# The sums of w2 in an FFN's input stage, and the ring of operands in its output stage

## The chip, the cores and the metric

One core of a Trainium2 chip runs the whole program in one launch. Its engines are TensorE (PE, matrix products), VectorE (DVE), ScalarE (ACT), GpSimd (POOL) and SyncE (SP); in this kernel SP issues nearly all DMAs, on one queue. Each engine works through its own instructions in order, and engines wait for each other by semaphores. The metric is the device time of one execution in microseconds (us); times before are the median of three runs.

## The reference

One layer of a two-pass (context and denoising) backbone. What matters here is its last third, the SwiGLU FFN over T = 1280 tokens (256 of the context, 1024 of the sample) with D = 1024 and D_FF = 2816:

```python
    x = x + g1 * rmsnorm(m, lp['g_post1'])
    h = rmsnorm(x, lp['g_pre2']) * (1.0 + sc2) + sh2
    f = (jax.nn.silu(h @ lp['ffn_w1']) * (h @ lp['ffn_w3'])) @ lp['ffn_w2']
    x = x + g2 * rmsnorm(f, lp['g_post2'])
```

All of it is float32. The token mixers ahead of it are the same before and after.

## The kernel before

Each float32 operand is split in two parts, a rounded high part and the rest, the low part, and each product is three matmuls: high x high, high x low, low x high. `split` does this: L65 casts the high part on ACT, L66 subtracts it on DVE (or POOL) to get the low part. So a low part is ready only after its high part.

Both stages of the FFN use Strassen's scheme in Winograd's form: seven products of blocks instead of eight, with sums of blocks before and after.

The *input stage*, `ffn_in`, goes over the 22 column tiles of D_FF in 11 pairs f. Per pair there are two halves, one for w1 and one for w3. A half is one call of `products` (matmuls L1347 for the seven products, 512 wide, and L90 to L92 for the remaining 256 tokens, about 134 matmuls in all); the adds that take its products out of PSUM are DVE's L1352, on tiles `t`. `w_raw` loads the weights (L1294), `w_sums` forms their sums for the next half (L1313, L1315 and L1322 on DVE, L1324 on POOL). After a pair, the activations and their seven sums go to DRAM in `actd` (stores L1417, L1448, L1449).

The second operand of the output stage also needs sums, those of w2. They don't depend on anything computed: `w2_sums(f, q)` loads two tiles of 256 KB (L1460) into the pool `tmp`, makes four DVE operations of 128 x 256 (L1462 to L1465) on them and stores both to `w2t` in DRAM (L1467). The pool `tmp` has two buffers, so a call's loads wait for the stores of the call before. There are 22 calls, two per pair; in the code both stand between the halves of their pair. A scheduler orders each engine's instructions by its own estimate of when they can run, so that an instruction written late can be placed early.

The *output stage*, `ffn_out`, has seven products of 11 steps, one step per pair, called 0, 1, 4, 5, 3, 6 and last 2. A step takes one tile pair `op` (high and low, 640 columns of activations and 512 of w2) and makes 15 matmuls (L1504), three for each of five PSUM banks `pg` and `pm`. `operands` makes these tiles: load both parts into `raw` (L1494 from `actd`, L1495 from w2 or `w2t`; three buffers), then `split`. Steps 0 and 1 of product 0 are loaded early and in parts through another pool, s4. The pool `op` has 22 tiles, that is 11 steps. Between products the banks are emptied: ACT copies them to the accumulators after product 0 (L1517) and product 1, DVE adds after the others.

The last product holds all its 11 steps (`xs`) and goes bank by bank, so that each bank's rows can be finished by `final` while the next runs: gate row (`gate_row`, L1285), the residual x1d (load L1577, into s4), the norm and the store of the output.

Of the kernel before, what the change touches and what calls it, by code (L numbers as in the profile page):

```python
# [11 lines left out]
F32R = mybir.dt.float32r  # L12
# [29 lines left out]
class Builder:  # L42
# [1291 lines left out]
    def products(self, ops, w, t3, func11, early=False):  # L1334
# [44 lines left out]
        product(c, "s4", "b22", False)  # L1379
        add(u2, u2, c)  # L1380
        yield d

    def ffn_in(self, given):
# [4 lines left out]
        for f in range(0, FT, 2):  # L1388
            early = not f
            if raw:  # L1390
                wa = self.w_sums(raw)
# [24 lines left out]
            def out(i, src, cols=slice(0, 512)):  # L1416
                nc.sync.dma_start(self.actd[f // 2][:, i, cols], src)  # L1417

            for q in range(2):
                self.w2_sums(f // 2, q)  # L1420
            if not early:
                tb = three()
                pb = self.products(ops, w1, tb, mul11)
            *_, d = pb
            out(0, s11)
            tt = nc.vector.tensor_tensor
# [23 lines left out]

    def w2_sums(self, f, q):


        nc = self.nc
        tt = nc.vector.tensor_tensor
        src = self.a["w2"][2 * f * P:(2 * f + 2) * P, :].rearrange("(i p) (h q c) -> i q p h c", i=2, h=2, q=2)
        dst = self.w2t[f].rearrange("p (i j) (q c) -> i q p j c", i=2, q=2)
        x = [self.tmp() for _ in range(2)]
        for i in range(2):
            nc.sync.dma_start(x[i].rearrange("p (h c) -> p h c", h=2), src[i, q])  # L1460
        (b11, b12), (b21, b22) = ([y[:, :256], y[:, 256:]] for y in x)
        tt(b11, b12, b11, ALU.subtract)  # L1462
        tt(b12, b22, b12, ALU.subtract)
        tt(b22, b22, b11, ALU.subtract)
        tt(b21, b21, b22, ALU.subtract)  # L1465
        for i in range(2):
            nc.sync.dma_start(dst[i, q], x[i].rearrange("p (j c) -> p j c", j=2))  # L1467

    def ffn_out(self):
# [12 lines left out]
        def operands(i, b, early=False):  # L1482
            for f in range(FT // 2):
                hi, lo = (self.opp.tile([P, HALF + 512], F32R, tag="op", bufs=22, name=self.nm("op")) for _ in range(2))
                ca, cb = slice(0, HALF), slice(HALF, HALF + 512)
                if early and f < 2:
                    for src, c in ((self.actd[f][:, i], ca), (b[f], cb)):
                        raw = self.s4()
                        n = c.stop - c.start
                        nc.sync.dma_start(raw[:, :n], src)  # L1490
                        self.split(raw[:, :n], hi[:, c], lo[:, c])
                else:
                    raw = self.opp.tile([P, HALF + 512], F32, tag="raw", bufs=3, name=self.nm("raw"))
                    nc.sync.dma_start(raw[:, ca], self.actd[f][:, i])  # L1494
                    nc.sync.dma_start(raw[:, cb], b[f])  # L1495
                    self.split(raw, hi, lo)
                yield hi, lo
# [18 lines left out]
        for x, y in zip(B[0], ps):  # L1516
            acopy(x, y)  # L1517
        product(1, w2(1, first), ps, False)
        for x, y in zip(A[0], ps):
            acopy(x, y)  # L1520
# [11 lines left out]
        product(6, w2(1, second), ps, False)  # L1532
        g2s = [self.gate_row(1, s) for s in range(2)]
        for j, (t, y) in enumerate(zip(HALVES[0], ps)):
            add(A[1][j], A[1][j], y)
            self.final(t, acc[t], g2s[t // 8])
        ps = banks()
        xs = list(operands(2, t4))
        for j, t in enumerate(HALVES[1]):
# [34 lines left out]
    def final(self, t, acc, g2):  # L1574
        nc = self.nc
        x = self.s4()
        nc.sync.dma_start(x, self.x1d[t * P:(t + 1) * P, :])  # L1577
        rs = self.tiny.tile([P, 1], F32, tag="rs", bufs=6, name=self.nm("rs"))
# [126 lines left out]
```

## Time and profile before

| | us |
|---|---|
| median of three runs | 1661.93 (1661.32 to 1664.87) |
| the profiled execution | 1657.5 |
| its span in the trace | 1655.6 |
| PE busy in the span | 1511.2 (91%) |
| DVE busy | 1048.9 (63%) |
| ACT busy | 667.6 (40%) |
| mean granted clock of PE | 0.962 of full speed |

The profiled execution is 4.4 us faster than the median, and 1.9 us of it lie outside the span. The FFN takes the second half of the span: input stage from about 784 us to 1363.33, output stage from there to the end.

A row of a timeline gives start, duration, engine, line, operation and tiles, and in brackets how long the engine idled before it and what ended that. A matmul's duration overlaps that of the next, so starts tell the rate. A row of waits gives the waiting instruction, what it waited for, the total, how many times and the longest. Idle time counts only on the engine that the others wait for; here that is PE.

### The profile page before, as it was taken

To read this page: it belongs to the slowest core of one execution; us is meant where nothing else is said; L and a number is where in the kernel's file an instruction comes from. 1 tells how busy PE (TensorE), PEld (TensorE's weight loads), DVE (VectorE), ACT (ScalarE), POOL (GpSimd) and SP (SyncE) were. 2 spreads that over 40 slices of the span, in tenths; PEclk is the share of its full clock that TensorE was granted. 3 is DMA by queue.
4 is the path that set the end of the run, shared out by engine and by line. 5 is a ranking of instruction groups with operands and counts; after the bars stand their busy time and mean duration, and the time that the engine had idled before them with its cause. 6 is when DMAs were issued, how large, how long until landed. Compare 5 with 4: busy or idle time off the path is not lost.

```text
span 1655.6 us, 23292 instructions
## 1 busy us (share of the span) xinstructions
PE 1511.2 (91%) x8493; PEld 1245.3 (75%) x8493; DVE 1048.9 (63%) x1762; ACT 667.6 (40%) x1224; POOL 415.9 (25%) x416
## 2 busy tenths in 40 slices
PE   5999998889989979984988989999999998799997
PEld 2688778677677767873777778888888886688886
DVE  7776568997388996469666665555455534534555
ACT  5754244554456667455221222222222213433341
POOL 2333236555045665344010101101011000000003
PEclk9999998999999989996999999999999999999999
DMA  8434562444512454631566553222232338755544
GB/s 323 142 125 139 170 182 80 140 138 146 195 64 83 147 180 155 227 112 49 159 198 200 161 175 107 82 87 76 84 101 84 104 96 286 231 171 173 174 140 165
DMA packets 163226, 242.17 MB, mean 146 GB/s; under 512 B 34613, under 2 KB 97407, under 8 KB 162984
## 3 DMA queue, kind: packets, MB, share of 16 engines
q1 hardware_dynamic: 163112, 240.69, 44.8%
q8 instruction: 67, 1.10, 0.3%
q14 instruction: 47, 0.39, 0.1%
HBM read 169.05 MB, written 71.58 MB: 145 GB/s over the span
## 4 chain that ended last, share of the span: by engine, by line
PE 46%; DMA 11%; DVE 9%; issue 3%; ACT 3%; POOL 2%; SPq 1%; DVEq 0%; POOLq 0%; ACTq 0%
PE pg L1347 13%; PE pg L1504 7%; PE pm L1504 7%; PE pm L1347 5%; DMA tmp<-in_w 4%; DMA w2t<-tmp 4%; PE pg L90 2%; PE pg L92 2%; PE pg L91 2%; PE pm L92 2%; PE pm L90 2%; PE pm L91 2%; DMA raw<-in_w 2%; PE pm L1042 1%; DMA s<-in_wfm 1%
## 5 line engine op out<-in xcount | busy, mean ns | idle before, releaser
L66 DVE TENSOR_TENSOR op<-raw,op 128x1152 fp32r<-128x1152 f32 x75 | 101.8, 1358 | 122.3 <-ACT op L65 121.8
L90 PE MATMUL pg<-hh,s 128*128 128x512 f32 (+1 forms) x432 | 158.0, 367 | 3.9 <-ACT s L65 3.9
L92 PE MATMUL pg<-hh,s 128*128 128x512 f32 (+1 forms) x432 | 154.9, 363 | 7.1 <-DVE s L66 7.1
L91 PE MATMUL pg<-hl,s 128*128 128x512 f32 (+1 forms) x432 | 155.8, 361 | 0.6 <-POOL hl L204 0.6
L65 ACT CAST op<-raw 128x1152 fp32r<-128x1152 f32 x75 | 87.1, 1161 | 158.2 <-PE pg L1504 65.3
L1324 POOL TENSOR_TENSOR sr<-s,s 128x512 f32<-128x512 f32 x22 | 28.7, 1307 | 473.0 <-DVE sr L1322 447.1
L1347 PE MATMUL pg<-hh,su 128*128 128x512 f32 x352 | 121.7, 407 | 14.9 <-DVE t L1352 10.9
L65 ACT CAST su<-sr 128x512 fp32r<-128x512 f32 x88 | 53.9, 619 | 194.9 <-POOL sr L1324 98.9
L1504 PE MATMUL pg<-op,op 128*128 128x512 f32 x396 | 124.6, 397 | 5.2 <-DVE op L66 5.2
L65 ACT CAST s<-s 128x1024 fp32r<-128x1024 f32 (+2 forms) x67 | 69.6, 1038 | 136.9 <-DMA s<-in_w 101.2
L1347 PE MATMUL pg<-b1h,s 128*128 128x512 f32 x352 | 118.9, 400 | 5.5 <-DVE tmp L1565 4.5
L98 POOL TENSOR_TENSOR rs<-rs,mhalf 128x1 f32<-128x1 f32 x40 | 30.0, 753 | 368.5 <-DVE rs L97 367.5
L1504 PE MATMUL pm<-op,op 128*128 128x512 f32 x374 | 116.2, 392 | 0.0
L66 DVE TENSOR_TENSOR s<-s,s 128x1024 fp32r<-128x1024 f32 (+2 forms) x67 | 84.8, 1266 | 31.2 <-ACT s L65 20.6
L90 PE MATMUL pm<-hh,s 128*128 128x256 f32 x352 | 99.7, 283 | 0.0
L91 PE MATMUL pm<-hl,s 128*128 128x256 f32 x352 | 99.7, 283 | 0.0
L92 PE MATMUL pm<-hh,s 128*128 128x256 f32 x352 | 99.6, 283 | 0.0
L92 PEld LDWEIGHTS pg<-hh,s 128*128 128x128 f32 x432 | 82.6, 191 | 21.3 <-DVE s L66 8.5
L90 PEld LDWEIGHTS pg<-hh,s 128*128 128x128 f32 x432 | 82.9, 192 | 19.3 <-ACT s L65 5.4
L1347 PEld LDWEIGHTS pg<-hh,su 128*128 128x128 f32 x352 | 68.2, 194 | 32.8 <-DVE t L1352 12.1
L91 PEld LDWEIGHTS pg<-hl,s 128*128 128x128 f32 x432 | 82.9, 192 | 12.8 <-POOL hl L204 0.9
L1504 PEld LDWEIGHTS pg<-op,op 128*128 128x128 f32 x396 | 76.0, 192 | 21.8 <-DVE op L66 6.0
(352 smaller groups left out, 4095.7 us busy)
## 6 DMA issues: line engine op xcount, KB each, us to landing
s<-in_wmod SPq DMA_DIRECT2D x48, 512.0 KB, 4.8
raw<-actd SPq DMA_DIRECT2D x75, 320.0 KB
s<-in_w SPq DMA_DIRECT2D x44, 512.0 KB, 4.3
actd<-t SPq DMA_DIRECT2D x66, 256.0 KB, 2.5
tmp<-in_w SPq DMA_DIRECT2D x44, 256.0 KB, 3.2
w2t<-tmp SPq DMA_DIRECT2D x44, 256.0 KB, 2.5
raw<-w2t SPq DMA_DIRECT2D x44, 256.0 KB, 3.3
s<-in_wfm SPq DMA_DIRECT2D x18, 512.0 KB, 4.7
```

Of the source, the lines that this page charges most:

```text
L65: nc.scalar.copy(hi, src)
L66: (eng or nc.vector).tensor_tensor(lo, src, hi.bitcast(F32), ALU.subtract)
L90: mm(ps, lh, rh, start=start, stop=False)
L91: mm(ps, lh, rl, start=False, stop=False)
L92: self.last = mm(ps, ll, rh, start=False, stop=stop).ins
L98: nc.gpsimd.tensor_tensor(out, out, self.mhalf[:, :cols], ALU.pow)
L1042: nc.tensor.matmul(ps[32 * r:32 * r + 32, ci * 4 * wide:(ci + 1) * 4 * wide], kk[:, c * P + 32 * r:c * P + 32 * r + 32], qb[:, :, i0:i0 + ...
L1324: pt(s3, a1[:, c], a2[:, c], ALU.subtract)
L1347: self.last = mm(ps, l[:, k], r[:, k], start=start and k == 0 and i == 0, stop=stop and k == 3 and i == 2, skip_group_check=True).ins
L1504: mm(ps, l, r, start=start and i == 0, stop=stop and i == 2, skip_group_check=True)
```

## The change

- `w2_sums` is cut in two: `w2_load` takes the buffers and issues the loads, `w2_sums` does the sums and the stores.
- In the input stage one call of the sums stands per half, for the pair before, and is held (`issue_after`) behind the last add of a product (`self.added`). The loads are held behind the last store to `actd` (`self.sent`), one call ahead of their sums.
- The two calls of the last pair move into `ffn_out`: its first load stands behind product 0's instructions in the code, its sums and the second load behind product 1's.
- The pool `op` shrinks from 22 tiles to 10, a ring of five steps; the first six steps of the last product get 12 tiles of their own (`oq`).
- The gate rows, the operands of the last product and the x1d loads of `final` are held behind the last load of `raw` that was written before them.

```diff
@@ products
-        add(u2, u2, c)
+        self.added = add(u2, u2, c).ins
@@ ffn_in
+            if not early:
+                with self.tc.issue_after(self.sent):
+                    w2 = self.w2_load(f // 2 - 1, 0)
...
-                nc.sync.dma_start(self.actd[f // 2][:, i, cols], src)
-
-            for q in range(2):
-                self.w2_sums(f // 2, q)
+                self.sent = nc.sync.dma_start(self.actd[f // 2][:, i, cols], src).ins
+
+            if not early:
+                with self.tc.issue_after(self.added):
+                    self.w2_sums(*w2)
+                with self.tc.issue_after(self.sent):
+                    w2 = self.w2_load(f // 2 - 1, 1)
             if not early:
                 tb = three()
                 pb = self.products(ops, w1, tb, mul11)
             *_, d = pb
+            if not early:
+                with self.tc.issue_after(self.added):
+                    self.w2_sums(*w2)
@@ w2_load, w2_sums
+    def w2_load(self, f, q):
+        x = [self.tmp() for _ in range(2)]
         src = self.a["w2"][2 * f * P:(2 * f + 2) * P, :].rearrange("(i p) (h q c) -> i q p h c", i=2, h=2, q=2)
+        for i in range(2):
+            self.nc.sync.dma_start(x[i].rearrange("p (h c) -> p h c", h=2), src[i, q])
+        return f, q, x
+
+    def w2_sums(self, f, q, x):
...
-        x = [self.tmp() for _ in range(2)]
-        for i in range(2):
-            nc.sync.dma_start(x[i].rearrange("p (h c) -> p h c", h=2), src[i, q])
@@ ffn_out
-                hi, lo = (self.opp.tile([P, HALF + 512], F32R, tag="op", bufs=22, name=self.nm("op")) for _ in range(2))
+                tag, n = ("oq", 12) if i == 2 and f < 6 else ("op", 10)
+                hi, lo = (self.opp.tile([P, HALF + 512], F32R, tag=tag, bufs=n, name=self.nm(tag)) for _ in range(2))
...
-                    nc.sync.dma_start(raw[:, cb], b[f])
+                    self.sent = nc.sync.dma_start(raw[:, cb], b[f]).ins
...
+        last = [self.w2_load(FT // 2 - 1, 0)]
         product(1, w2(1, first), ps, False)
+        for q in range(2):
+            self.w2_sums(*last.pop())
+            if not q:
+                last.append(self.w2_load(FT // 2 - 1, 1))
...
-        g2s = [self.gate_row(1, s) for s in range(2)]
+        with self.tc.issue_after(self.sent):
+            g2s = [self.gate_row(1, s) for s in range(2)]
+            xs = list(operands(2, t4))
...
-        xs = list(operands(2, t4))
@@ final
-        nc.sync.dma_start(x, self.x1d[t * P:(t + 1) * P, :])
+        with self.tc.issue_after(self.sent):
+            nc.sync.dma_start(x, self.x1d[t * P:(t + 1) * P, :])
```

The lines move with it: the loads of w2 are L1464 after the change, the four sums L1473 to L1476, the stores L1478, the copies after product 0 L1529; the adds stay L1352.

How the instructions stand on the engines at three places. First DVE in the middle of the input stage before the change; `t` from `pg` or `pm` are the adds, `sr` and `su` sums and splits of the next weights, `tmp` the sums of w2.

```order
L1352 TENSOR_TENSOR t_1329_7988<-t_1329_7988,pg_8001 128x512
L1462 TENSOR_TENSOR tmp_9024<-tmp_9024 128x256
L1463 TENSOR_TENSOR tmp_9024<-tmp_9025,tmp_9024 128x256
L1352 TENSOR_TENSOR t_1330_7989<-t_1330_7989,pm_8002 128x512
L1464 TENSOR_TENSOR tmp_9025<-tmp_9025,tmp_9024 128x256
L1465 TENSOR_TENSOR tmp_9025<-tmp_9025 128x256
L1313 TENSOR_TENSOR sr_8391<-s_1374_8229 128x512
L1315 TENSOR_TENSOR sr_8393<-sr_8391,s_1373_8227 128x512
L1352 TENSOR_TENSOR t_1336_7995<-t_1334_7993,pg_8059 128x512
```

And DVE in one half of the stage after the change.

```order
L1352 TENSOR_TENSOR t_1567_9646<-t_1567_9646,pg_9652 128x512
L1313 TENSOR_TENSOR sr_10027<-s_1593_9832 128x512
L1352 TENSOR_TENSOR t_1568_9647<-t_1568_9647,pm_9653 128x512
L1473 TENSOR_TENSOR tmp_9606<-tmp_9606 128x256
L66 TENSOR_TENSOR su_9827<-sr_9814,su_9826 128x512
L1474 TENSOR_TENSOR tmp_9606<-tmp_9607,tmp_9606 128x256
L1315 TENSOR_TENSOR sr_10029<-sr_10027,s_1592_9830 128x512
L1475 TENSOR_TENSOR tmp_9607<-tmp_9607,tmp_9606 128x256
L1476 TENSOR_TENSOR tmp_9607<-tmp_9607 128x256
L1352 TENSOR_TENSOR t_1597_9845<-t_1596_9844,pg_9848 128x512
```

Before, a call's first sums stand ahead of a product's last add; now all four stand behind that add and ahead of the first add of the next half.

Second, DVE where the output stage begins, before the change: the last add, the activations' sums (`t`), and the first pieces of the low part of step 0 (`op`).

```order
L1352 TENSOR_TENSOR t_1941_12345<-t_1941_12345,pm_12349 128x512
L1433 TENSOR_TENSOR t_1912_12141<-t_1912_12141,t_1941_12345 128x512
L1437 TENSOR_TENSOR t_1940_12344<-t_1912_12141,t_1913_12142 128x512
L1438 TENSOR_TENSOR t_1941_12345<-t_1940_12344,pj_12143 128x512
L1440 TENSOR_TENSOR t_1912_12141<-pj_12143,t_1912_12141 128x512
L1439 TENSOR_TENSOR t_1942_12346<-t_1911_12140,t_1941_12345 128x512
L66 TENSOR_TENSOR op_12538<-s_1965_12539,op_12537 128x640
```

The same place after the change, behind the same add.

```order
L1473 TENSOR_TENSOR tmp_12314<-tmp_12314 128x256
L1442 TENSOR_TENSOR t_1910_12125<-t_1910_12125,t_1937_12319 128x512
L1474 TENSOR_TENSOR tmp_12314<-tmp_12315,tmp_12314 128x256
L1446 TENSOR_TENSOR t_1936_12318<-t_1910_12125,t_1911_12126 128x512
L1475 TENSOR_TENSOR tmp_12315<-tmp_12315,tmp_12314 128x256
L1447 TENSOR_TENSOR t_1937_12319<-t_1936_12318,pj_12127 128x512
L1449 TENSOR_TENSOR t_1910_12125<-pj_12127,t_1910_12125 128x512
L1476 TENSOR_TENSOR tmp_12315<-tmp_12315 128x256
L1448 TENSOR_TENSOR t_1938_12320<-t_1909_12124,t_1937_12319 128x512
L1473 TENSOR_TENSOR tmp_12770<-tmp_12770 128x256
L1474 TENSOR_TENSOR tmp_12770<-tmp_12771,tmp_12770 128x256
L66 TENSOR_TENSOR op_12518<-s_1961_12519,op_12517 128x640
```

Six sums of w2 now stand ahead of the first piece of the low part, the last two of them on tiles (`tmp_12770`, `tmp_12771`) whose buffers the four before have to leave first.

Third, ACT at the end of product 0 before the change: the casts of product 1 from its first step on, then the copies that empty product 0's banks.

```order
L65 CAST op_12790<-raw_12792 128x1152
L65 CAST op_12812<-raw_12814 128x1152
L65 CAST op_12834<-raw_12836 128x1152
L65 CAST op_12856<-raw_12858 128x1152
L65 CAST op_12878<-raw_12880 128x1152
L65 CAST op_12900<-raw_12902 128x1152
L65 CAST op_12922<-raw_12924 128x1152
L65 CAST op_12944<-raw_12946 128x1152
L1517 COPY acc_12526<-pg_12532 128x512
L1517 COPY acc_12527<-pm_12533 128x512
L65 CAST op_12966<-raw_12968 128x1152
L1517 COPY acc_12528<-pg_12534 128x512
```

ACT there after the change, again from product 1's first cast.

```order
L65 CAST op_12774<-raw_12776 128x1152
L65 CAST op_12796<-raw_12798 128x1152
L65 CAST op_12818<-raw_12820 128x1152
L65 CAST op_12840<-raw_12842 128x1152
L1529 COPY acc_12506<-pg_12512 128x512
L1529 COPY acc_12507<-pm_12513 128x512
L1529 COPY acc_12508<-pg_12514 128x512
L1529 COPY acc_12509<-pm_12515 128x512
L1529 COPY acc_12511<-pg_12516 128x512
```

Four casts stand ahead of the copies instead of eight, and all five copies are together.

## Rows read from the trace of the kernel before

**Rows 1.** Windows: start:end, length, busy (instructions) by engine, clock, DMA share, GB/s.
```profile
785.00:984.14 199.14, 179.12 (x891) 149.81 (x891) 127.71 (x219) 43.29 (x66) 20.78 (x15) 0.96 0.57 180
984.14:1363.33 379.19, 379.19 (x1981) 322.85 (x1980) 197.95 (x287) 97.39 (x141) 36.19 (x28) 1.00 0.27 90
1363.33:1421.00 57.67, 42.02 (x167) 33.38 (x166) 29.39 (x27) 20.65 (x20) 0.00 (x0) 0.90 0.84 275
1430.00:1606.00 176.00, 176.00 (x778) 145.80 (x777) 80.69 (x68) 63.32 (x59) 0.00 (x0) 1.00 0.58 178
```

**Rows 2.** Windows ahead of the stage, PE's matmuls of line L1347 alone (first busy).
```profile
748.00:755.00 7.00, 6.98 (x24) 5.49 (x24) 0.78 0.19 75
780.00:785.00 5.00, 3.78 (x8) 2.48 (x8) 0.50 0.36 105
```

**Rows 3.** Waits of PE from 785 to 984.14: total, times, longest.
```profile
PE pg L1347 <- DVE t L1352: 19.1, 9, 5.3
PE pg L1347 <- ACT t L1354: 0.9, 1, 0.9
```

**Rows 4.** Timeline of PE: in the input stage, and around product 0.
```profile
968.85 1.05 PE L1347 MATMUL pg<-hh,su 128*128 128x512 f32 x2
...
1368.99 1.22 PE L1504 MATMUL pg<-op,op 128*128 128x512 f32 x2 [4.34 <-DVE op L66]
...
1375.90 0.61 PE L1504 MATMUL pg<-op,op 128*128 128x512 f32 x2
1377.96 0.50 PE L1504 MATMUL pg<-op 128*128 128x512 f32 x1 [1.44 <-ACT op L65]
...
1410.90 0.61 PE L1504 MATMUL pg<-op,op 128*128 128x512 f32 x2
1420.50 0.80 PE L1504 MATMUL pg<-op 128*128 128x512 f32 x1 [8.98 <-ACT acc L1517]
```

**Rows 5.** Groups of DVE's instructions by form, 780 to 985: busy, mean ns | idle before.
```profile
L1465 DVE TENSOR_TENSOR tmp<-tmp 128x256 f32<-128x256 f32 x22 | 12.9, 587 | 0.4
...
L1462 DVE TENSOR_TENSOR tmp<-tmp 128x256 f32<-128x256 f32 x22 | 10.6, 484 | 36.7 <-DMA tmp<-in_w 36.7
```

**Rows 6.** Landing times by source: L1460 (loads of w2), then L1467 (stores).
```profile
DMA to landing us min/median/max: 3.1/3.2/4.6
...
DMA to landing us min/median/max: 2.1/2.5/7.3
```

**Rows 7.** Timeline of ACT: the first copy that empties product 0's banks.
```profile
1419.87 0.58 ACT L1517 COPY acc<-pg 128x512 f32<-128x512 f32 x1
```

**Rows 8.** Timeline of the undisturbed part: two adds of DVE, one matmul of PE.
```profile
1118.01 0.68 DVE L1352 TENSOR_TENSOR t<-t,pg 128x512 f32<-128x512 f32 x1
...
1121.76 0.39 PE L1347 MATMUL pg<-hh,su 128*128 128x512 f32 x1
...
1141.58 0.69 DVE L1352 TENSOR_TENSOR t<-t,pg 128x512 f32<-128x512 f32 x1 [2.34 <-PE pg L1347]
```

**Rows 9.** Timeline of DVE: the last add of the input stage.
```profile
1363.53 0.69 DVE L1352 TENSOR_TENSOR t<-t,pm 128x512 f32<-128x512 f32 x1 [1.36 <-PE pm L1347]
```

**Rows 10.** Timeline of SP's queue: gates and part of the x1d loads.
```profile
1363.29 1.88 SPq L1285 DMA_DIRECT2D gate<-gated  x4
...
1375.60 2.49 SPq L1577 DMA_DIRECT2D s<-x1d  x4
```

**Rows 11.** Landing times of L1495 (raw): 1363 to 1425, then 1430 to 1606.
```profile
DMA to landing us min/median/max: 3.5/4.7/6.6
...
DMA to landing us min/median/max: 3.2/3.4/4.6
```

**Rows 12.** The page's groups: the two halves of a split in the output stage.
```profile
L66 DVE TENSOR_TENSOR op<-raw,op 128x1152 fp32r<-128x1152 f32 x75 | 101.8, 1358 | 122.3 <-ACT op L65 121.8
...
L65 ACT CAST op<-raw 128x1152 fp32r<-128x1152 f32 x75 | 87.1, 1161 | 158.2 <-PE pg L1504 65.3
```

**Rows 13.** Timeline of PE: its last matmuls.
```profile
1645.98 0.61 PE L1504 MATMUL pm<-op,op 128*128 128x512 f32 x2
```

More of the change, by code (lines that the diff above doesn't have):

```diff
@@ L1449, in ffn_in @@
             nc.sync.dma_start(self.actd[f // 2][:, 3:, last], sq.rearrange("p (i c) -> p i c", i=4))
-    def w2_sums(self, f, q):
-        nc = self.nc
-        tt = nc.vector.tensor_tensor
+    def w2_load(self, f, q):
+        x = [self.tmp() for _ in range(2)]
         src = self.a["w2"][2 * f * P:(2 * f + 2) * P, :].rearrange("(i p) (h q c) -> i q p h c", i=2, h=2, q=2)
+        for i in range(2):
+            self.nc.sync.dma_start(x[i].rearrange("p (h c) -> p h c", h=2), src[i, q])
+        return f, q, x
+    def w2_sums(self, f, q, x):
+        tt = self.nc.vector.tensor_tensor
         dst = self.w2t[f].rearrange("p (i j) (q c) -> i q p j c", i=2, q=2)
-        x = [self.tmp() for _ in range(2)]
-        for i in range(2):
-            nc.sync.dma_start(x[i].rearrange("p (h c) -> p h c", h=2), src[i, q])
         (b11, b12), (b21, b22) = ([y[:, :256], y[:, 256:]] for y in x)
@@ L1466, in w2_sums @@
         for i in range(2):
-            nc.sync.dma_start(dst[i, q], x[i].rearrange("p (j c) -> p j c", j=2))
+            self.nc.sync.dma_start(dst[i, q], x[i].rearrange("p (j c) -> p j c", j=2))
     def ffn_out(self):
```

## The prediction

> **What bounds the kernel now.** I read the table of windows first. The input stage of the FFN falls into two parts [rows 1]: 199.14 us up to 984.14, in which PE is busy for only 179.12, and then 379.19 us in which PE is busy throughout at a granted clock of 1.00. The second part is 15 halves (a half is the seven products of w1 or of w3 for one pair), so an undisturbed half takes 379.19 / 15 = 25.28 us. The first part holds the seven halves ahead of them. Seven times 25.28 is 177.0; 32 of its 512-wide matmuls had already run before 785 [rows 2], which at full speed are 32 x 0.23 = 7.4 us; so it should take 169.6 us and takes 199.1, 29.5 too many. PE's waits name the culprit [rows 3]: 19.1 us in nine waits for DVE's adds of PSUM (L1352), 0.9 for a copy of ACT. The other 9.5 us are work at the lower clock: just after the longest wait, 5.3 us, two matmuls take 1.05 us [rows 4], and the mean clock of the part is 0.96, two levels mixed, 1.2 and 2.4 GHz.
>
> DVE is late because sums of w2 stand in front of its adds, in order: the 22 rounds of w2_sums all lie in this first part, and their first operations idle until a load lands (36.7 us ahead of L1462, with only 10.6 us of work [rows 5]). The tmp pool has two buffers, so each round is a load, the sums, a store and only then the next load: 3.2 and 2.5 us and the sums [rows 6]. An add queued behind such a round waits with it, and PE waits for the add.
>
> The output stage is full on PE from 1430 us on [rows 1]. Its first product is not: between 1363.33 and 1421 PE is busy 42.02 of 57.67 us, with the DMA engines at 0.84. Three waits stand out in PE's timeline [rows 4]: 4.34 us for the first low parts, 1.44 for a cast, and 8.98 before the second product, which wants its banks emptied by ACT. ACT's first copy begins at 1419.87 [rows 7], although the first product ended at 1411.5 [rows 4], because eight casts of the next product stand ahead of it in ACT's order and each waits for its load.
>
> **The change part by part.** (1) *Sums spread, one round per half.* In DVE's order the four sums of a round now stand behind the last add of a product, and their loads are issued about half a pair (25 us) earlier; a load lands in 3.2 us, 4.6 at most [rows 6]. So the 19.1 us of waits of [rows 3] go, and with them the low clock they cause: at most 29.5. I leave the ACT copy (0.9) and one wait of 1.6, a little under the mean of the nine, and count **27 us**. Bounds: 20 (the waits go, the clock stays) and 29.
>
> What is late next? The sums join the second part of the stage, where DVE idles. The first and the last of the four take 0.48 and 0.59 us beside other work [rows 5]; I take 0.34 on the queue, where its start overlaps its neighbour. In one half three of them stand before an add that ends at 1118.70, while PE starts the product that waits for it at 1121.76 [rows 8]: 3.0 us of room, 1.0 used. In the other half four stand before the add at 1141.58, ahead of which DVE idles 2.34 us [rows 8]: 1.4 used. With 0.59 each it would be 1.8 and 2.4, just at the edge. Their loads and stores are 23 MB in 579 us, 40 GB/s, added to 90 GB/s at a DMA share of 0.27 [rows 1]. I count nothing; if a busier stretch eats that room, 15 halves by 0.25 us are 4 us lost.
>
> (2) *The entry of the output stage.* The sums of the next-to-last pair's second part now stand behind the add of 1363.53 [rows 9] on DVE, and then the first two sums of the last pair, ahead of the low part of step 0. What they need is a chain. DVE is through with the earlier round at 1364.2 + 4 x 0.43 + 4 x 0.61 = 1368.4 (sums and adds at what they take when queued); its store lands 2.5 later (1370.9); the next load waits for that buffer and lands 3.2 us and 0.4 of issue later (1374.5); two sums and the first pieces of the split follow (2.0). PE then resumes at about **1376.5 instead of 1368.99**, 7.5 us later: a new wait on the path. By the rows it lies between 1376.0 (store 2.1, load 3.1) and 1382.7 (store 7.3, load 4.6) [rows 6]. SP's raws of the later steps stand behind the same load and leave at about 1371.5.
>
> I take the medians since the load of this moment falls: four gate loads at 1363.29 and four x1d loads at 1375.60 [rows 10], 3 MB, are gone from here. The Trainium skill's page "DMA: Bandwidth & Descriptors", section "Latency and other measured facts", goes further: it gives an HBM access latency of 0.2 us on average and 2 us under high load, so that a lighter load makes the fixed cost smaller. By it store and load could each be up to 1.8 us shorter, PE would resume at 1373 and the total would be 3.6 us lower. Of this case's 44 loads and 44 stores none is more than 0.4 us below its median [rows 6], so the trace doesn't bear it out.
>
> (3) *The rest of product 0.* From 1368.99 to 1376.5 run the 25 matmuls that complete steps 0 and 1, restart at low clock included [rows 4]; the other nine steps take 15 matmuls of 0.226 us each (176.00 / 778 [rows 1]), 3.4 us. With nothing late, product 0 ends at 1376.5 + 7.5 + 9 x 3.4 = 1414.6. Can the loads keep up? A step is 576 KB; nine steps of product 0, four of product 1 and ten transfers of w2 are 10.3 MB, at 275 GB/s [rows 1] 37 us from about 1372 on: 1409. They can, with some 5 us in hand. The ring of five lets ACT cast only four steps of product 1 ahead of the copies, so these come as soon as the product ends, and the wait of 8.98 us goes. Product 1 starts at 1414.6 instead of 1420.50, and without a second slow restart: the first one's 25 matmuls took 7.5 us for 5.65, 1.9 lost; I take 1.2 for this one, whose wait ends with its banks coming free one by one. Gain: **7 us**, the new wait included. Bounds: 0 (the entry at 1382.7, or loads behind) and 9 (all 1.9, the entry half a microsecond sooner).
>
> (4) *A ring of five from there to the end of product 6.* A load takes 3.4 us (4.6 at most) [rows 11] and a step's two splits 1.16 + 1.36 = 2.5 [rows 12]; with issue, 8 us at most. Five steps of 3.4 us with one in use leave 13.6. Nothing counted; 4 us is the price if one boundary falls short.
>
> (5) *Late loads.* Gates and x1d now come behind the last product's raws, some 2 us into that product by my walk of SP's order. Ten loads of 512 KB take 2 us each at 275 GB/s, 20 us of a product that lasts 11 x 3.4 = 37. PE's last matmuls at 1645.98 [rows 13] and the 9 us from their end to that of the span stay. Nothing counted; 4 us lost if the finals bunch up.
>
> Sum: 27 + 7 = 34 us. The profiled execution took 1657.5 (span 1655.6) and lies 4.4 us below the median of the runs; its own time becomes 1623.5. Against the median, 1661.9, I predict **1628**.
>
> **The rivals.** *The entry eats the gain of the fill.* Its store queues with actd's stores and lands like the slowest, 7.3 us; or bytes bind the fill after all (w2's last pair adds 2 MB where the late loads take 3 away). For it: DMA at 0.84 there. Then (3) gives 0, with (1) between 20 and 27: 1661.9 less 20 to 27 is 1635 to 1642. Chance 0.17.
>
> *The entry is short*: the two loads come earlier than I walk them (store and sums overlap), PE resumes at 1371 to 1373, and (1) gives its full 29: 6 to 12 us below the forecast, 1616 to 1622. Chance 0.05. The skill's rule above is a way to half of this.
>
> *The ring starves at product boundaries.* ACT's copies or DVE's adds (five of 0.7 us) delay the splits, and five boundaries lose 3 to 5 us each, 14 to 27 in all: 1642 to 1655. Against it: the 5 us in hand in (4). Chance 0.09.
>
> *The sums stay in PE's way.* The loads, now behind a pair's last store in SP's order, land after DVE gets to the sums, the adds wait as before and only the fill gains: 1655, give or take 4. Against it: the lead in (1). Chance 0.03.
>
> *Slower: each step waits for its load.* Three raw buffers hold three steps; each is busy for a load, 2.5 us of splits and about 0.4 of issue. Three steps of PE are 10.2 us, so a load over 7.3 us starves PE, which a ring of eleven hides for a while and one of five does not. To eat all 34 us in the 66 steps of the ring takes 0.52 us a step, a load of 8.9 us. The slowest of the fill was 6.6, of later ones 4.6 [rows 11]. 1664 to 1680. Chance 0.04.
>
> **How the numbers follow.** Forecast, 1622 to 1634 (all of (1)'s and (3)'s inner spread): 0.62. The others are 0.17, 0.05, 0.09, 0.03 and 0.04; together 1. The range 1619 to 1643 takes in the forecast, the first rival and half of the second, about 0.81. About 0.2% is what a measurement of this kernel can tell from no change. Faster by more than that: all but the slower rival and a third of the one before it, 0.95; within 0.2%, 0.01; slower, 0.04.
>
> **What would show it.** After the change PE's waits for DVE's adds in the input stage should sum to under 3 us, and that stage's first part last about 172 us. Just behind the stage PE should wait some 12 us for the first low parts, not 4, and then not 2 us before product 1, which starts 51 us after the stage's end (57 before); from there PE is full to the end of the last product. I am wrong if adds of the second part become late, if the wait at the entry passes 18 us, or if PE waits for casts within products 1 to 6.

## The result, and the profile after

The changed kernel takes 1623.15 us (median of 1622.12 to 1625.48) against 1661.82 in the same comparison: a ratio of 0.9766, 95% interval 0.9749 to 0.9782, or 38.7 us less. The profiled execution took 1622.27, its span is 1620.5 (1657.5 and 1655.6 before). Two later comparisons, shown below, gave 0.979 (0.9765 to 0.9815) and 0.9817 (0.9798 to 0.9835), 34.7 and 31.9 us. The traces say 31.3, by the stretches that the change touches; how these numbers fit together is the last point of the explanation.

First the windows, in the columns of [rows 1]: the input stage in two parts, the stretch up to the second product, the output stage, and from the last product's first matmul to the span's end.

```profile
776.90:976.90 200.00, 200.00 (x1037) 170.59 (x1038) 118.68 (x179) 56.00 (x80) 24.93 (x19) 0.99 0.34 111
976.90:1329.91 353.01, 353.01 (x1846) 300.81 (x1844) 201.10 (x321) 89.11 (x130) 33.66 (x26) 1.00 0.38 127
1329.91:1381.50 51.59, 38.40 (x161) 31.29 (x160) 27.70 (x35) 15.94 (x15) 0.00 (x0) 0.87 0.76 245
1395.00:1571.00 176.00, 176.00 (x778) 145.82 (x777) 82.18 (x70) 64.92 (x59) 0.00 (x0) 1.00 0.60 187
...
1569.68:1620.50 50.82, 37.88 (x166) 30.71 (x164) 38.22 (x45) 16.97 (x27) 21.36 (x14) 0.91 0.70 252
```

The same last stretch of the kernel before:

```profile
1609.04:1655.60 46.56, 37.56 (x166) 30.79 (x164) 29.17 (x39) 11.71 (x21) 17.20 (x14) 0.93 0.39 147
```

The input stage is full on PE throughout, 553.0 us from its first matmul at 776.90 to 1329.91, where it was 582.7 (780.67 to 1363.33). The DMA share is 0.34 to 0.38 throughout the stage instead of 0.57 and then 0.27 [rows 1]: the w2 traffic is spread. All waits of PE from 785 to 1606 are one row, where [rows 3] and [rows 4] had the nine waits for adds, the cast and the copies:

```profile
PE pg L1516 <- DVE op L66: 13.2, 1, 13.2
```

This is the entry of the output stage. In PE's timeline it lies here:

```profile
1330.83 0.40 PE L1516 MATMUL pg<-op 128*128 128x512 f32 x1
1344.42 1.22 PE L1516 MATMUL pg<-op,op 128*128 128x512 f32 x2 [13.19 <-DVE op L66]
```

And DVE's timeline shows what it did in that time: the last sum of the earlier round, two waits for a load of w2, and then the first piece of the low part of step 0.

```profile
1334.13 0.42 DVE L1476 TENSOR_TENSOR tmp<-tmp 128x256 f32<-128x256 f32 x1
1334.46 0.68 DVE L1448 TENSOR_TENSOR t<-t,t 128x512 f32<-128x512 f32 x1
1338.32 0.42 DVE L1473 TENSOR_TENSOR tmp<-tmp 128x256 f32<-128x256 f32 x1 [3.17 <-DMA tmp<-in_w]
1342.27 0.43 DVE L1474 TENSOR_TENSOR tmp<-tmp,tmp 128x256 f32<-128x256 f32 x1 [3.53 <-DMA tmp<-in_w]
1342.61 0.82 DVE L66 TENSOR_TENSOR op<-s,op 128x640 fp32r<-128x640 f32 x1
```

SP's queue at that time, store and load issues of w2:

```profile
1334.88 0.55 SPq L1464 DMA_DIRECT2D tmp<-in_w  x1
1335.53 0.55 SPq L1478 DMA_DIRECT2D w2t<-tmp  x1
...
1339.00 0.55 SPq L1464 DMA_DIRECT2D tmp<-in_w  x1
```

The second store leaves at 1335.53, the load that waits for it at 1339.00, and its data are there at 1342.27: the chain of the prediction, link by link.

At the end of product 0 the copies come at once. The first one, of ACT's timeline (1419.87 before [rows 7]):

```profile
1380.54 0.58 ACT L1529 COPY acc<-pg 128x512 f32<-128x512 f32 x1
```

That is 50.6 us after the input stage's end instead of 56.5. In PE's timeline product 1 then starts 52.8 us after it, where it was 57.2 (1420.50 [rows 4]), and the last product 239.8 us after it:

```profile
1382.68 0.39 PE L1516 MATMUL pg<-op 128*128 128x512 f32 x1
...
1569.68 0.39 PE L1516 MATMUL pm<-oq 128*128 128x512 f32 x1
```

Before, the last product started 245.7 us after the stage's end:

```profile
1609.04 0.39 PE L1504 MATMUL pm<-op 128*128 128x512 f32 x1
```

The last lines are PE's last matmuls and DVE's last add of PSUM:

```profile
1607.04 0.61 PE L1516 MATMUL pm<-op,op 128*128 128x512 f32 x2
...
1611.51 0.68 DVE L1491 TENSOR_TENSOR acc<-acc,pm 128x512 f32<-128x512 f32 x1
```

PE ends at 1607.65, but DVE comes to its result only at 1611.51, 3.9 us later, because it is busy. Before, PE ended at 1646.59 [rows 13] and DVE took the result at once:

```profile
1646.63 0.69 DVE L1480 TENSOR_TENSOR acc<-acc,pm 128x512 f32<-128x512 f32 x1 [2.08 <-PE pm L1504]
```

So the tail behind PE's end is 12.8 us instead of 9.0. In sum, by stretches: 29.6 us gained in the input stage, 5.9 from there to the last product's first matmul (245.7 to 239.8), 4.2 lost from that matmul to the end of the span (46.6 to 50.8): 31.3.

### The profile page after: what moved, and what is told of

The parts are those of the page before. It is cut to its first block, busy times and chain, and to the rows that moved or that the text cites. A ratio compares the mean times of both kernels' runs of the same rounds, so it can differ in the third digit from the quotient of the medians.

```text
span 1620.5 us, 23277 instructions
## 1 busy us (share of the span) xinstructions
PE 1495.8 (92%) x8493; PEld 1236.3 (76%) x8493; DVE 1045.6 (65%) x1762; ACT 668.6 (41%) x1224; POOL 419.7 (26%) x416
## 4 chain that ended last, share of the span: by engine, by line
PE 56%; DVE 8%; DMA 3%; issue 3%; POOL 2%; ACT 2%; SPq 0%; POOLq 0%; DVEq 0%; ACTq 0%
PE pg L1347 19%; PE pm L1347 7%; PE pg L1516 6%; PE pm L1516 6%; PE pg L92 3%; PE pg L90 3%; PE pg L91 3%; PE pm L90 3%; PE pm L92 3%; PE pm L91 3%; DMA raw<-w2t 1%; PE pm L1042 1%; POOL rs L98 1%; DVE b L942 0%; POOL acc L1611 0%
## 5 line engine op out<-in xcount | busy, mean ns | idle before, releaser
L66 DVE TENSOR_TENSOR op<-raw,op 128x1152 fp32r<-128x1152 f32 x69 | 93.7, 1357 | 104.7 <-ACT op L65 104.7
L65 ACT CAST op<-raw 128x1152 fp32r<-128x1152 f32 x69 | 80.1, 1161 | 151.8 <-PE pg L1516 73.2
L1516 PE MATMUL pg<-op,op 128*128 128x512 f32 x372 | 115.7, 393 | 13.2 <-DVE op L66 13.2
L98 POOL TENSOR_TENSOR rs<-rs,mhalf 128x1 f32<-128x1 f32 x40 | 31.3, 787 | 363.8 <-DVE rs L97 362.8
L1347 PE MATMUL pg<-b1h,s 128*128 128x512 f32 x352 | 119.0, 400 | 4.5 <-DVE tmp L1583 4.5
L1347 PE MATMUL pg<-hh,su 128*128 128x512 f32 x352 | 118.5, 397 | 3.9 <-ACT su L65 3.9
L65 ACT CAST su<-sr 128x512 fp32r<-128x512 f32 x88 | 54.2, 619 | 163.7 <-POOL sr L1324 57.2
L66 DVE TENSOR_TENSOR s<-s,s 128x1024 fp32r<-128x1024 f32 (+2 forms) x67 | 86.0, 1284 | 32.9 <-ACT s L65 18.5
L1516 PE MATMUL pm<-op,op 128*128 128x512 f32 x338 | 105.0, 392 | 0.0
L1352 DVE TENSOR_TENSOR t<-t,pg 128x512 f32<-128x512 f32 x66 | 45.3, 686 | 82.6 <-PE pg L1347 76.2
L1516 PEld LDWEIGHTS pg<-op,op 128*128 128x128 f32 x372 | 70.5, 190 | 28.3 <-DVE op L66 13.6
L91 PEld LDWEIGHTS pg<-hl,s 128*128 128x128 f32 x432 | 82.3, 190 | 12.4 <-POOL hl L204 0.9
```

Source lines behind the costliest of these rows:

```text
L65: nc.scalar.copy(hi, src)
L66: (eng or nc.vector).tensor_tensor(lo, src, hi.bitcast(F32), ALU.subtract)
L91: mm(ps, lh, rl, start=False, stop=False)
L98: nc.gpsimd.tensor_tensor(out, out, self.mhalf[:, :cols], ALU.pow)
L1347: self.last = mm(ps, l[:, k], r[:, k], start=start and k == 0 and i == 0, stop=stop and k == 3 and i == 2, skip_group_check=True).ins
L1352: add = lambda out, x, y: nc.vector.tensor_tensor(out, x, y, ALU.add)
```

## The experiments

The table holds four lengths of each trace, read from its timelines: the input stage (from its first matmul after 770 us to the first matmul of the output stage), the first copy that empties product 0's banks, counted from the stage's end, the rest from the stage's end to the span's end, and of that rest the part from the last product's first matmul (the 991st of the output stage, since a product has 165) to the span's end. The last column counts the splits (L66) that DVE does after its first add of product 6. Times are medians, with the kernel before on the same chip beside them; e1 to e4, the next four and the last four are one comparison each.

| kernel | median us | before | input stage | first copy | output stage | last product | splits late |
|---|---|---|---|---|---|---|---|
| before | 1661.8 | | 582.7 | 56.5 | 292.3 | 46.6 | 2 |
| the change | 1623.2 | 1661.8 | 553.0 | 50.6 | 290.6 | 50.8 | 5 |
| e1_only_sums | 1625.8 | 1654.7 | 553.1 | 55.5 | 291.4 | 46.6 | 2 |
| e2_only_ring | 1646.4 | 1654.7 | 582.8 | 41.9 | 282.6 | 51.6 | 4 |
| e3_only_late | 1654.2 | 1654.7 | 581.8 | 54.1 | 291.0 | 46.6 | 2 |
| e4_entry_free | 1619.1 | 1654.7 | 552.5 | 45.5 | 283.3 | 50.1 | 5 |
| r5_change_again | 1622.0 | 1656.6 | 553.0 | 50.7 | 290.7 | 50.9 | 5 |
| r5_entry_free | 1619.9 | 1656.6 | 552.5 | 46.4 | 286.5 | 50.8 | 5 |
| e5_last_spread | 1618.7 | 1656.6 | 552.5 | 50.2 | 286.3 | 46.6 | 2 |
| e6_both | 1612.5 | 1656.6 | 552.8 | 45.0 | 279.3 | 46.6 | 2 |
| r11_change | 1626.3 | 1658.2 | 553.1 | 50.5 | 290.3 | 50.7 | 5 |
| e8_no_late | 1623.8 | 1658.2 | 553.2 | 50.3 | 289.8 | 50.3 | 4 |
| r12_both | 1615.0 | 1658.2 | 552.5 | 47.4 | 283.3 | 46.6 | 2 |
| e9_both_no_late | 1618.7 | 1658.2 | 552.8 | 48.4 | 285.5 | 46.6 | 2 |

**One part alone.** Three kernels each make one part of the change.

e1_only_sums is the changed kernel with these parts taken back:

```diff
-                tag, n = ("oq", 12) if i == 2 and f < 6 else ("op", 10)
+                hi, lo = (... tag="op", bufs=22 ...)
-        with self.tc.issue_after(self.sent):
-            g2s = [self.gate_row(1, s) for s in range(2)]
-            xs = list(operands(2, t4))
+        g2s = [self.gate_row(1, s) for s in range(2)]
...
+        xs = list(operands(2, t4))
...
-        with self.tc.issue_after(self.sent):
-            nc.sync.dma_start(x, self.x1d[t * P:(t + 1) * P, :])
+        nc.sync.dma_start(x, self.x1d[t * P:(t + 1) * P, :])
```

> The sums of w2 spread as in the change, but the ring of eleven steps and the early gate and x1d loads of before. If the input stage's gain comes from the sums alone, that stage takes 553 us from its first matmul after 776.9 to its end, as with the whole change (582.7 before), with no PE wait for adds. The entry wait of about 13 us comes with it. Copies after product 0 stand behind six casts. Theory: 29.6 us gained in the stage, 0 to 5 lost in the fill, the tail behind PE's end at 9.0 us as before: 1632 to 1637. Rival, the sums need the other parts (DMA traffic of the gates and x1d loads slows the stores): the stage itself over 560 us and the total over 1640.

The stage takes 553.1 us, so the sums alone make the whole gain there. The waits of PE from 785 to 1420:

```profile
PE pg L1515 <- DVE op L66: 12.7, 1, 12.7
PE pg L1515 <- ACT acc L1528: 3.4, 1, 3.4
```

The entry wait comes with the sums, and with a ring of eleven a wait of 3.4 us for the copies is left. The output stage gains 0.8 us in all. The time, 28.9 us under its before, is the forecast's size (25 to 30).

e2_only_ring is the kernel before with the ring:

```diff
-                hi, lo = (... tag="op", bufs=22 ...)
+                tag, n = ("oq", 12) if i == 2 and f < 6 else ("op", 10)
+                hi, lo = (... tag=tag, bufs=n ...)
```

> Before, with only the ring of five steps and the six separate steps of the last product. Theory: only four casts of product 1 stand ahead of the copies, so the wait of 9.0 us before product 1 goes while the low parts of step 0 still come after 4.3 us: product 1 starts 47 to 50 us after the input stage's end (57 before), about 9 us gained; the input stage keeps its 20 us of waits. If the ring is what made the tail behind PE's end 12.9 us instead of 9.0 (five splits of the last product pushed behind the end of product 6), 4 of it are lost: 1655 to 1657. If the late loads made the tail, it stays at 9.0: 1651 to 1653. Rival, a ring of five starves: waits for casts within products 1 to 6 and no gain.

The first copy comes at 41.9 us and product 1 starts at 44.0, earlier than the theory had it. The last product starts 14.7 us earlier than before (231.0 us after the stage's end), and from there to the span's end 5.0 are lost again: 9.7 gained in the output stage. PE's waits from 1362 to 1600 are one row, the old entry wait plus a fifth of a microsecond:

```profile
PE pg L1505 <- DVE op L66: 4.5, 2, 4.3
```

Through products 1 to 6 a ring of five does not starve. Why 44 and not 47? SP's timeline has the first load of raw at 1366.70, 4.7 us after the stage's end; before, it left at 1372.87, 9.5 us after, and SP's longest wait in that stretch was for it:

```profile
SPq L1494 <- DMA actd<-t: 4.8, 1, 4.8
```

In the ring's trace no wait of that size stands ahead of a raw load:

```profile
1366.70 0.99 SPq L1495 DMA_DIRECT2D raw<-actd  x1
```

With fewer tiles in front of it, raw lies elsewhere in memory, where it need not wait for the last activations' stores; that reading of the cause is argued, not tried.

The ring also pays at the other end. Its trace has a wait of PE in the last product:

```profile
1609.61 1.11 PE L1505 MATMUL pm<-op,op 128*128 128x512 f32 x2 [1.88 <-DVE rs L97]
```

The row names a small operation (L97) that ended at the same moment. The matmul reads a low part, and DVE had just finished a late split, behind an operation that took 3.41 us:

```profile
1604.87 3.41 DVE L1591 SCALAR_TENSOR_TENSOR acc<-acc,rs,gate 128x1024 f32<-128x1024 f32 x1 [0.38 <-POOL rs L98]
1608.21 1.35 DVE L66 TENSOR_TENSOR op<-raw,op 128x1152 fp32r<-128x1152 f32 x1
```

So at the end of the last product the late splits hold up PE as well.

e3_only_late is the kernel before with only the gates, the last product's operands and the x1d loads held behind the last raw load.

> Before, with only the gate, last-product and x1d loads held behind the last raw load. Theory: product 0 has the DMA engines to itself, but ten casts now stand ahead of the copies, so product 1 still waits for its loads: it starts 52 to 57 us after the input stage's end, 0 to 5 us gained. If the late loads make the tail long (x1d awaited, DVE and POOL adding at the same time), the tail behind PE's end is about 13 us: total 1660 to 1664. If the ring makes it, 9.0: 1656 to 1660.

```diff
-                    nc.sync.dma_start(raw[:, cb], b[f])
+                    self.sent = nc.sync.dma_start(raw[:, cb], b[f]).ins
...
+        with self.tc.issue_after(self.sent):
             g2s = [self.gate_row(1, s) for s in range(2)]
+            xs = list(operands(2, t4))
...
-        xs = list(operands(2, t4))
...
+        with self.tc.issue_after(self.sent):
             nc.sync.dma_start(x, self.x1d[t * P:(t + 1) * P, :])
```

Nothing of note: 0.5 us, ratio 0.999 (0.9973 to 1.0008). Product 1 still waits for its copies, 10.9 us, and the tail behind PE's end stays at 9.0. So the late loads neither help the fill much nor make the tail longer.

**The entry.** e4_entry_free is the change with one line pinned:

```diff
-        last = [self.w2_load(FT // 2 - 1, 0)]
+        with self.tc.issue_after(self.sent):
+            last = [self.w2_load(FT // 2 - 1, 0)]
```

> The whole change, with the last pair's first w2 loads held behind product 0's last raw load, so that their sums stand behind the low parts of steps 0 and 1 on DVE. Theory: the entry wait of 13.2 us falls to 5 or 6 (only four sums of the pair before remain there), product 1 starts 44 us after the input stage's end instead of 51, and the total falls by 6 to 8 us to 1615 to 1617. Rival, the fill is bound by bytes: PE waits for casts of later steps instead, and the total stays at 1620 to 1623.

```profile
1338.13 1.22 PE L1516 MATMUL pg<-op,op 128*128 128x512 f32 x2 [5.31 <-DVE op L66]
```

PE's timeline shows 5.3 us instead of 13.2, at 6.6 us after the stage's end instead of 14.5. The first copy comes at 45.5, 5.1 us earlier; PE then waits 0.9 for the copies, which it did not in the change. The output stage is 7.3 us shorter in this trace. Run again beside the whole change:

> The whole change again, on the same chip as the three beside it. By the stretches of the traces so far the change is worth 29.6 us in the input stage and 5.5 in the first products, less 3.9 behind PE's end: 31 us below the kernel before. The 38.7 of the first comparison holds some 4 us more, which lay ahead of the changed code in the profiled runs. Theory: 30 to 33 us below before. Rival, the change is worth 38 us and the profile of before was a lucky one: 37 to 40 below.

> The whole change with the last pair's w2 loads behind product 0's last raw load. Against the whole change beside it: 6 to 8 us less by the traces (entry wait 13.2 to 5.3 us). Rival: under 3 us, the fill being bound by its loads.

The whole change is 34.7 us below before, between the two theories; its trace repeats the stretches to 0.1 us. Without the long entry wait it is 2.1 us faster than with it, within the scatter of the runs (1617.6 to 1623.47 against 1621.12 to 1625.52), and 4.2 in the output stage by the traces: the rival's size by the medians, between the two by the traces. That is less than the first trace had shown: here PE waits 1.8 us for the copies, and takes 188.7 us from there to the last product's start where the first trace has 187.1. The entry wait is real, but once it is gone the copies and the casts ahead of them stand close behind it.

**The tail.** e5_last_spread takes the last product's six steps with tiles of their own out of the crowd at the end:

```diff
-        def product(i, b, ps, start, early=False):
+        def product(i, b, ps, start, early=False, more=()):
...
+                if f in more:
+                    xs.append(next(xg))
...
+        xs, xg = [], operands(2, t4)
         product(0, w2(0, first), ps, True, True)
...
-        product(3, t1, ps, True)
+        product(3, t1, ps, True, more=(2, 5, 8))
-        product(6, w2(1, second), ps, False)
+        product(6, w2(1, second), ps, False, more=(0, 3, 6))
...
-            xs = list(operands(2, t4))
+            xs += xg
```

> The whole change, with the loads and splits of the last product's first six steps (which have their own twelve tiles) taken one per three steps during products 3 and 6, instead of all behind product 6. Theory: the longer tail comes from the ring: the last product's splits are late, five of them (1.35 us each) fall behind product 6's end on DVE, three more than before, and DVE is what the tail waits for. Spread, two fall there, and the tail behind PE's end goes from 12.9 to about 9 us: 3 to 5 us below the whole change. Rival, the late x1d loads make the tail: then it stays at 12 to 13.

PE's last matmuls and DVE's last add in its timeline:

```profile
1602.99 0.61 PE L1516 MATMUL pm<-op,op 128*128 128x512 f32 x2
...
1603.64 0.69 DVE L1491 TENSOR_TENSOR acc<-acc,pm 128x512 f32<-128x512 f32 x1 [1.54 <-PE pm L1516]
```

DVE waits for PE again, and the tail is 9.0 us. Two splits are left behind product 6 instead of five; 3.2 us faster than the change beside it, 4.4 in the output stage by the traces. The x1d loads are still held, but the first of them leaves 1.7 us ahead of the last product here and 6.4 us into it in the change. That this is not what shortens the tail is shown by e2, and by e8 below: they load x1d early, and their last product is as long as the change's. The ring makes the tail.

e6_both has the edits of e4 and e5, and r12_both is the same kernel in the next comparison, with the change beside it as r11_change.

> Both of the two edits: the last pair's w2 sums behind the low parts of steps 0 and 1, and the last product's first six steps spread over products 3 and 6. If the two places are independent, the gains add: 10 to 12 us below the whole change, the input stage full, entry wait 5 to 6 us, tail about 9 us. Rival, the extra loads in products 3 and 6 starve the ring of five and take back 3 to 5 us.

> The two edits on the change, again: 8 to 11 us below the whole change beside it.

9.4 and 11.3 us below the change beside it; against before 0.9725 (0.9697 to 0.9752) and 0.9748 (0.9725 to 0.977). It beats both kernels. Its waits of PE from 785 on are, in the first trace, 5.3 us at the entry and 0.2 for the copies; in the second the copies cost 2.8.

**The late loads, inside the change.** e8_no_late and e9_both_no_late are the change and e6 with gates and x1d loaded as early as before:

```diff
-        with self.tc.issue_after(self.sent):
-            g2s = [self.gate_row(1, s) for s in range(2)]
-            xs = list(operands(2, t4))
+        g2s = [self.gate_row(1, s) for s in range(2)]
+        xs = list(operands(2, t4))
...
-        with self.tc.issue_after(self.sent):
-            nc.sync.dma_start(x, self.x1d[t * P:(t + 1) * P, :])
+        nc.sync.dma_start(x, self.x1d[t * P:(t + 1) * P, :])
```

(In e9 the line with `xs` is `xs += xg`.)

> The whole change, for the chip of the run beside it: 34 to 36 us below before; stage 553 us, product 1 some 51 us after its end, tail 12.7 us.

> The whole change without its late loads: gates and x1d are loaded early as before, spread sums and ring stay. Theory: with the ring alone product 1 began 41.9 us after the input stage with these loads in the fill, so bytes don't bind the fill and the late loads bring nothing: entry 13 to 15 us, product 1 at 50 to 53, total within 2 us of the whole change; the tail stays long, since the ring makes it. Rival: with the last pair's w2 in the fill as well, these 3 MB bind: product 1 at 54 to 57, total 3 to 6 us above the whole change.

> The two edits on the change, without its late loads. Theory: within 2 us of the run with them; x1d early may even free the adds at the end: 0 to 2 below. Rival: the loads bind the fill: product 1 at 48 to 51 instead of 45 and 3 to 5 us above.

Without late loads the change takes 2.5 us less (1623.8 against 1626.3), 0.5 in the output stage by the traces: no difference that these runs can tell. The entry wait is 12.4, the first copy at 50.3. In e6 the same edit takes 3.7 us more, 2.2 in the output stage by the traces, with a wait of 3.3 us for the copies instead of 2.8. So late loads do nothing while the entry wait stands; with it gone they may be worth some 2 us, which the spread between the output stages of e6's two traces (4.0 us) leaves open.

## Why the prediction was right, point by point

It gave 1628, range 1619 to 1643; measured 1623.15. The parts, against the stretches:

(1) *The sums*: forecast 27, bounds 20 and 29; 29.6 measured, by e1 all from this part. The two waits that were kept back (0.9 and 1.6) did not come: no wait for an add is left in 553 us. The undisturbed half of 25.28 us was the right yardstick (22 halves are 556; the stage takes 553.0 since 24 matmuls, 5.5 us, ran ahead of it and its first ones are slow). The room on DVE was larger than worked out: the four sums take 0.42 us each on average in the new place; the last of them had 0.59:

```profile
L1476 DVE TENSOR_TENSOR tmp<-tmp 128x256 f32<-128x256 f32 x19 | 8.0, 422 | 0.3
```

(2) *The entry*: 7.5 us later than before was forecast, 13.2 us after the stage's end; measured 14.5. The chain is the right one; its store was sized too short. It queues behind a load on SP and leaves 1.0 us after its sums, for which the walk had nothing, and it lands 3.4 us after its issue, where the walk had the median of 2.5. The landing time of that one store:

```profile
DMA to landing us min/median/max: 3.4/3.4/3.4
```

The other links nearly cancel: the sums are done 0.4 us sooner, load and issue take 3.3 us instead of 3.6, the last two sums and the split 2.1 instead of 2.0. Over the whole trace the landings became steadier, L1464 first, then L1478:

```profile
DMA to landing us min/median/max: 2.9/3.2/3.3
...
DMA to landing us min/median/max: 2.1/2.4/3.4
```

Against [rows 6] the medians are the same (3.2; 2.4 for 2.5) and only the slowest are gone (4.6, 7.3). The Trainium skill's page "DMA: Bandwidth & Descriptors", section "Latency and other measured facts", has the fixed cost fall with the load on HBM; by it the entry would have come earlier than the forecast. It came later, and the medians did not move, with the DMA share of the stage down from 0.57 to between 0.34 and 0.38: at this size the trace does not bear the rule out in the medians, only in the slowest. The one store on the path speaks neither way: it landed as slowly as any, but behind the stage, where the share is 0.76.

(3) *The rest of the fill*: product 1 was to start 51.3 us after the stage's end; it starts at 52.8, where it was 57.2. From PE's restart to product 1 it is 38.3 us, and the sum had 38.1, so the entry's 1.3 is nearly the whole difference. The slow restart that went is worth 1.5 more up to the last product's first matmul, where the sum had 1.2: 5.9 gained by then, where 7 was forecast. The ring's own part was sized rightly too: 7 net and 7.5 for the entry make 14.5, and e2, the ring without the longer entry, reaches the last product 14.7 us earlier than before. By these figures the moved sums take 8.8 of it back.

(4) and (5) *Ring and late loads, each counted at nothing*: this is the step that failed. PE is indeed never short of a step, from product 1 to product 6. But from the last product's first matmul to the span's end there are 50.8 us instead of 46.6, so 4.2 are lost. (5) names that price ("if the finals bunch up") and puts it down to the late loads. Their walk was short, too (the first x1d load leaves 6.4 us into the last product, not 2), but they are not the cause: e3 and e5 have them and take 46.6, e2 and e8 don't and take 51.6 and 50.3. All seven traces with the ring and without e5's edit have four or five splits late and take 50.1 to 51.6; the other seven have two and take 46.6. The mechanism belongs to (4): a ring of five lets ACT and DVE run only five steps ahead, so the last product's splits (1.35 us each) come after product 6, when DVE has ten rows to finish. The sum asked whether PE gets its operands in time, and never whether DVE has room for the splits there. DVE's busy time in the last stretch shows it: 38.2 us of 50.8, against 29.2 of 46.6. Not all of that is splits. In each of the seven longer traces two operations of DVE take some 3.4 us instead of 1.2 or 1.3 beside an add of POOL (the last section shows one), in the others one does. e5's edit removes the late splits and the second such row together, so how the loss divides between them is open. Nor is PE always full in the last product: in r11_change it waits 1.4 us there, in e2 2.1.

So (2) to (5) give 1.7 us net where 7 was forecast, and (1) 2.6 more than forecast: 31.3 for 34. That the first comparison gave 38.7 has another reason, next.

*The rivals.* The first one came half true: the output stage as a whole gains almost nothing, but the entry is only 1.3 us late, and the rest is lost behind product 6. The short entry did not come. The starving ring and the sums in PE's way are excluded by the single row of PE's waits; the raw loads of the fill land in 4.4 us at most from w2 and in 5.8 from `actd`, so the slower rival, which needs loads over 7.3 us, did not come either.

*The total.* Against the one trace of before, the three traces of the change are 31.3, 31.2 and 31.5 us shorter (input and output stage together, 874.9 before; 843.6, 843.8 and 843.4); by the medians it is 38.7, 34.7 and 31.9. Of the first comparison's 7.4 us of difference, 3.8 lie ahead of the code that changed, where every kernel here has the same instructions in the same order: the stage's first matmul comes at 780.7 in the trace of before and 776.9 in that of after, and over the fourteen traces anywhere from 773.8 to 785.5. The rest is that the profiled execution lies 4.3 us below its median before and 0.9 below it after; no trace shows where. The median of before itself went from 1654.7 to 1661.8 in four comparisons.

So there is some luck in the total, in two places. The 2.6 us by which (1) came out above its term cover half of the 5.3 that (2) to (5) fell short. And the scatter ahead of the change moved the measured time: 1661.8 less 31.3 would be 1630.5, which lies in the range as well, 2.5 us above the forecast instead of 4.9 below it.

## What to carry to other kernels

A transfer that feeds an in-order engine belongs one whole use ahead of it, and at the end of a stage one must look where the last of them now falls: here the moved sums took a new place at the head of the next stage and cost more than half of what the ring gained. In products 1 to 6 the smaller ring cost nothing on the engine that reads it, since it was never empty; look also at the engines that fill it, and what else they have to do when the last turn of the ring comes late. Compare stretches of the trace, not totals, when a change is worth less than the scatter of what lies ahead of it.

## What the runs showed of the hardware

The stretches repeat far better than the whole: the input stage took 552.5 to 553.2 us in eleven traces of kernels with spread sums, and 581.8 to 582.8 in three without, on more than one chip, while the 780 us ahead of it varied by 12 us with the same instructions in the same order. Between the two ends of that range (e5 and r11) the lag of DVE's instructions grows in steps: 3.5 us by 94 us, still 3.9 at 401, 7.0 at 455, 9.7 at 610, 11.7 at 737. The granted clock in the two differs in places (0.96 and 0.93 from 500 to 640 us), but which event makes a step was not settled.

DVE beside POOL: the same operation of DVE took 1.28 us at 1592.08 and 3.42 at 1588.22, when POOL's add of 2.39 us had begun just before it. DVE's timeline, then POOL's:

```profile
1588.22 3.42 DVE L1609 SCALAR_TENSOR_TENSOR acc<-acc,rs,gate 128x1024 f32<-128x1024 f32 x1 [0.44 <-POOL rs L98]
1592.08 1.28 DVE L1609 SCALAR_TENSOR_TENSOR acc<-acc,rs,gate 128x1024 f32<-128x1024 f32 x1 [0.44 <-POOL rs L98]
```

```profile
1588.16 2.39 POOL L1611 TENSOR_TENSOR acc<-acc,s 128x1024 f32<-128x1024 f32 x1
```

3.42 is nearly the sum of the two, so DVE waited for POOL rather than shared with it. The Trainium skill's page "SBUF — State Buffer", section "SBUF: two separate sides", says that: the port pair that DVE and GpSimd share is an exclusive lock, and the later one blocks. The trace agrees. In a stretch where DVE is what the end waits for, such a row is some 2.1 us more work on DVE (3.42 less 1.28).
